# New x and block sums turned by DMA instead of TensorE at the inner boundaries of a two-layer encoder kernel, with the last tile's norm given priority and weight loads held behind the sums

## The chip, the cores and the metric

The kernel runs on one core of one Trainium2 chip. The metric is the device time of one execution in microseconds; before the change the median of three runs is 1997.66 us (1997.49 to 1998.72).

## What is computed

Two layers over x of 512 x 1024 float32; each layer is a feed-forward block ("f"), a token mixer ("m"), a second feed-forward block and a gated embedding block ("p"). Each ends in a layer norm of the sum of its input and its output, and that norm's result is the next block's x. In the reference, cut down:

```python
def reference(x, p, ...):
    for i in range(2):
        x = layer_norm(ALPHA * x + 0.5 * swiglu(x, ffn_w_in[i, 0], ffn_w_out[i, 0]), ...)
        x = layer_norm(ALPHA * x + token_mix(x, mix_w_in[i], ..., mix_w_out[i]), ...)
        x = layer_norm(ALPHA * x + 0.5 * swiglu(x, ffn_w_in[i, 1], ffn_w_out[i, 1]), ...)
        ple = sigmoid(x @ ple_w_gate[i] + ple_b_gate[i]) * (p[i] @ ple_w_proj[i])
        x = layer_norm(ALPHA * x + ple, ...)
    return x

def swiglu(x, w_in, w_out):                 # w_in 1024 x 5632, w_out 2816 x 1024
    gate, up = split(x @ w_in, 2)
    return (silu(gate) * up) @ w_out
```

## The kernel before, in words

The eight blocks run one after the other in the order f m f p, f m f p, so there are seven inner boundaries: f to m twice, m to f twice, f to p twice, p to f once. A Tile scheduler lists the instructions of each engine in a fixed order from the program and its priorities; on the chip each engine takes its own list in order and waits on semaphores. All loads and stores go through one queue, SP's, which also waits in order.

x stands in SBUF in four tiles of 128 tokens by 1024 (`x_tok`). A matmul needs x with the 1024 channels on the partitions, in two float16 parts whose sum is the float32 value: `xT`, high and low. A product is three matmuls, high by high, high by low, low by high (`mm3`, L270, L273, L274). So at each boundary every new tile of x is turned. Before the change that is done by `to_T` (L213): eight float32 128x128 transposes on TensorE (L224) into two PSUM banks `ps_t`, a copy on ScalarE to the high part (L229), a subtraction on VectorE for the low part (L230). `layer_norm` (L179) puts a tile on a list `pending`, and `flush` (L207) turns what is listed: the transposes of tile t stand on TensorE behind the output product of tile t+1, and those of the last tile in the next block.

A feed-forward block multiplies by Strassen's method in 2x2 blocks for hidden chunks 2 to 21 (`begin`, `step`), so it also needs four sums of blocks of x (`xS`, again two float16 parts). They are made from the transposed PSUM banks: a copy (L240), three to four subtractions (L246, L248), and `put_sums` (L255) with a copy on ScalarE (L262) and a subtraction on VectorE (L263). Chunks 0 and 1 use plain products; they are what TensorE has to do before the sums are there: `pg` and `pu` (the line of `project`), first for columns 0 to 384 of x (tiles 0 to 2), then for tile 3. The weight blocks of each chunk ("quad") are loaded to `f` (L470, L471), summed on VectorE (L484), and split in high and low by ScalarE (L141) and VectorE (L142) into `wq`. The output matrix comes in slabs `raw`, split by the same lines into `w`; `out_proj` (L492) runs per tile and group of chunks, ends in an eviction on VectorE (L517), and the norm of the tile follows (L185 to L197), with one small operation on GpSimd (L190). The last group of a feed-forward block has six chunks, that is 36 matmuls a tile.

The block p (L520) splits four slabs of `ple_w_gate` and one of `ple_w_proj` into `w`, multiplies tile by tile (`pgate`, then `pp`), and turns p itself by 16 TensorE transposes (`ps_p`, L550). Its slabs `w` lie in SBUF where the feed-forward block's buffers lay, so a split can wait for that block's last readers. In the mixer, `pv` (L653) is the first product, tile by tile.

Of the kernel before, what the change touches and what calls it, by code (L numbers as in the profile page):

```python
# [9 lines left out]
F16 = mybir.dt.float16  # L10
# [18 lines left out]

WS = 256.0  # L30
IWS = 1.0 / WS


class Block:
# [144 lines left out]
    def layer_norm(self, t, y, gb, last=False):  # L179

        nc = self.nc
        g, b = gb
        st = self.small.tile([P, 2, 6], F32, name="st")
        for h in range(2):
            nc.vector.bn_stats(st[:, h], y[:, h * 512 : (h + 1) * 512])  # L185
        mv = self.small.tile([P, 2], F32, name="mv")
        nc.vector.bn_aggr(mv, st.rearrange("p a b -> p (a b)"))
        rs = self.small.tile([P, 2], F32, name="rs")
        nc.vector.tensor_scalar(rs[:, 0:1], mv[:, 1:2], LN_EPS / ALPHA**2, None, op0=ALU.add)
        nc.gpsimd.tensor_tensor(rs[:, 1:2], rs[:, 0:1], self.mhalf[:, 0:1], op=ALU.pow)  # L190
        halves = [y[:, h * 512 : (h + 1) * 512] for h in range(2)]
        for h, yh in enumerate(halves):
            nc.vector.scalar_tensor_tensor(
                yh, yh, mv[:, 0:1], g[:, h * 512 : (h + 1) * 512], op0=ALU.subtract, op1=ALU.mult
            )
        for h, yh in enumerate(halves):
            nc.vector.scalar_tensor_tensor(  # L197
                yh, yh, rs[:, 1:2], b[:, h * 512 : (h + 1) * 512], op0=ALU.mult, op1=ALU.add
            )
# [13 lines left out]
    def to_T(self, xT, t, y, sums):  # L213
# [36 lines left out]
        if held is not None and t > 0:  # L250
            held.append(step)
        else:
            step()

    def put_sums(self, xS):  # L255

# [19 lines left out]
    def ffn(self, i, f, j, last=False):  # L276
# [7 lines left out]
        with ExitStack() as ctx:  # L284
# [37 lines left out]

            loads, loaded = [], []
            for m0, m1 in groups:
                loads += [lambda m=m: self.load_quad(w_in, m) for m in range(max(m0, 2), m1)]
                loads += [
                    lambda k=k, m=m0: (
                        self.load_rows(w_out, k, behind=self.chunks_end if first and m == 0 else None),
                        None,
                    ) for k in range(m0, m1, 2)  # L330
                ]

            def fetch(n):
                while loads and len(loaded) < n:
# [25 lines left out]
            for m in range(2):  # L360
                if m == 1:
                    self.put_sums(xS)
                ps = []
                for name, w in (("pg", wg), ("pu", wu)):
# [76 lines left out]
            for gi, (m0, m1) in enumerate(groups):  # L441
# [7 lines left out]
                wo = weights((m1 - m0) // 2)  # L449
                if gi == len(groups) - 1:  # L450
                    gb = self.ln_consts(i, j, self.w2, tag="w")
                for t in range(NT):
                    self.out_proj(
                        t, lambda q, m: hT[(m0 + m) // 2][:, q, m % 2], wo, m1 - m0,
# [1 line left out]
                    )  # L456
                    self.flush()
                    if gi == len(groups) - 1:
                        self.layer_norm(t, x[:, t], gb, last)

    def load_quad(self, w_in, m):


        nc = self.nc
# [5 lines left out]
        nc.sync.dma_start(f[:, 0:2], g)  # L470
        nc.sync.dma_start(f[:, 4:6], u)  # L471
        w = self.ring.tile([P, 2, 7, 4, P], F16, name="wq", tag="wq")

        def split(*slots):
# [45 lines left out]
    def ple(self, i, j, last=False):  # L520
        nc, ins, x, xT = self.nc, self.ins, self.x, self.xT
        self.xT = self.act.tile([P, 2, KD, S], F16, name="xT", tag="xT", bufs=2)
        with self.tc.tile_pool(name="ple", bufs=1, reuse_waits="tile") as pool, \
                self.tc.tile_pool(name="w1", bufs=5, reuse_waits="tile") as self.w1:
            pr = [self.t2("pr", (P, 2, 256)) for _ in range(2)]
            for h in range(2):
                nc.sync.dma_start(
                    pr[h], ins["p"][i, 0, 256 * h : 256 * h + 256].rearrange("(t p) e -> p t e", p=P)
                )
            wg = [self.load_rows(ins["ple_w_gate"][i], k, self.w1) for k in range(0, KD, 2)]  # L530
            wp = self.load_rows(ins["ple_w_proj"][i], 0, self.w1)
            bg = pool.tile([P, D], F32, name="bg")
            self.after(nc.sync.dma_start(bg, ins["ple_b_gate"][i : i + 1, :].to_broadcast([P, D])), self.loaded)
            gb = self.ln_consts(i, j, pool)
            pT = pool.tile([P, 2, 2, S], F16, name="pT")
            for t in range(NT):
                ts = slice(t * P, (t + 1) * P)
                pgs = [self.acc("pgate") for _ in range(2)]
                for h in range(2):
                    hs = slice(h * 512, (h + 1) * 512)  # L540
                    for m in range(KD):
                        self.mm3(
                            pgs[h], [xT[:, q, m, ts] for q in range(2)],
                            [wg[m // 2][:, q, m % 2, hs] for q in range(2)], m == 0, m == KD - 1,
                        )
                if t == 0:
                    for c in range(2):
                        ps = self.bank2("ps_p", (P, NT, P))
                        for tt in range(NT):
                            nc.tensor.transpose(  # L550
                                ps[:, tt], pr[tt // 2][:, tt % 2, c * P : (c + 1) * P], self.ident
                            )
                        hi = pT[:, 0, c].rearrange("p (t q) -> p t q", t=NT)
                        nc.scalar.activation(hi, ps, AF.Copy)
                        nc.vector.tensor_tensor(
                            pT[:, 1, c].rearrange("p (t q) -> p t q", t=NT), ps, hi,
                            op=ALU.subtract,
                        )
                self.flush()
                for h in range(2):  # L560
# [43 lines left out]
    def mix_body(self, i, j, last, pool):  # L604
# [7 lines left out]
        OFF_Q, OFF_K, OFF_V, OFF_Z, OFF_AB, OFF_SC = 768, 1280, 1792, 2304, 2816, 2824  # L612


        rows = self.t2("rows", (55, P))
        nc.sync.dma_start(rows[0:48], ins["gdn_conv_w"][i].rearrange("t (c p) -> (t c) p", p=P))
        nc.sync.dma_start(rows[48:54], ins["sc_conv_w"][i].rearrange("t (c p) -> (t c) p", p=P))
        nc.sync.dma_start(rows[54:55], ins["gdn_norm_w"][i : i + 1, :])
# [535 lines left out]
        for t in range(NT):  # L1154
            self.out_proj(t, lambda q, m: mT[:, q, m], wo, KD, IWS / ALPHA)
            self.flush()
            self.layer_norm(t, x[:, t], gb, last)

    def load_x(self):
        self.xT = self.act.tile([P, 2, KD, S], F16, name="xT", tag="xT", bufs=2)  # L1160
# [34 lines left out]
def encoder_block(ctx: ExitStack, tc: tile.TileContext, ins, out, stages="fmfp", layers=range(DEPTH)):  # L1195
# [2 lines left out]
    k.load_x()  # L1198
    for (i, j, s), following in zip(n, n[1:] + [None]):
        last = following is None  # L1200
        k.next_sums = not last and following[2] == "f"
        if s == "f":
            k.ffn(i, 0 if j == 0 else 1, j, last)
        elif s == "m":
# [25 lines left out]
```

## Time and profile before

| | |
|---|---|
| median of three runs | 1997.66 us |
| the profiled execution | 1997.14 us, span 1995.4 us |
| granted TensorE clock, mean over the span | 0.997 |
| VectorE busy | 76% of the span |
| ScalarE busy | 44% |
| bytes moved by DMA | 205.15 MB, 103 GB/s over the span |

The profile is of one execution. A row of the timeline has start, duration, engine, line, operation, output and inputs, size and count, and in brackets how long the engine had been idle and who released it. Matmuls overlap, so a matmul's own duration is longer than the step from its start to the next start; the step is what it costs. "PE" is TensorE, "PEld" its weight loads, "DVE" VectorE, "ACT" ScalarE, "POOL" GpSimd, "SPq" SP's queue.

### The profile page before, as it was taken

To read this page: it belongs to the slowest core of one execution; us is meant where nothing else is said; L and a number is where in the kernel's file an instruction comes from. 1 tells how busy PE (TensorE), PEld (TensorE's weight loads), DVE (VectorE), ACT (ScalarE), POOL (GpSimd) and SP (SyncE) were. 2 spreads that over 40 slices of the span, in tenths; PEclk is the share of its full clock that TensorE was granted. 3 is DMA by queue.
4 is the path that set the end of the run, shared out by engine and by line. 5 is a ranking of instruction groups with operands and counts; after the bars stand their busy time and mean duration, and the time that the engine had idled before them with its cause. 6 is when DMAs were issued, how large, how long until landed. Compare 5 with 4: busy or idle time off the path is not lost.

```text
span 1995.4 us, 33112 instructions
## 1 busy us (share of the span) xinstructions
PE 1951.3 (98%) x14058; PEld 1273.5 (64%) x14058; DVE 1521.9 (76%) x2347; ACT 868.1 (44%) x1294; POOL 69.9 (4%) x92
## 2 busy tenths in 40 slices
PE   8999999999999999999999999999999999999998
PEld 6677685545546677685467685854455466776853
DVE  8996766775679895869897877577756897967586
ACT  6454352454335453444264453424643364443430
POOL 1000000100000000000000000002000000000000
PEclk9999999999999999999999999999999999999999
DMA  8543320422162433334224343212222534333221
GB/s 243 181 127 106 86 86 14 117 56 64 65 197 79 148 106 106 106 120 148 92 85 127 106 126 84 66 55 78 53 86 80 174 97 136 106 106 85 96 74 43
DMA packets 245359, 205.15 MB, mean 103 GB/s; under 512 B 20846, under 2 KB 225500, under 8 KB 245212
## 3 DMA queue, kind: packets, MB, share of 16 engines
q1 hardware_dynamic: 245212, 203.05, 33.2%
q8 instruction: 110, 1.80, 0.4%
q14 instruction: 37, 0.30, 0.0%
HBM read 200.14 MB, written 2.88 MB: 102 GB/s over the span
## 4 chain that ended last, share of the span: by engine, by line
PE 75%; DVE 16%; ACT 6%; issue 2%; DMA 0%; POOL 0%; SPq 0%; DVEq 0%; ACTq 0%
PE po L274 7%; PE po L270 7%; PE po L273 7%; PE pA L270 6%; PE pA L273 6%; PE pA L274 6%; DVE wq L142 3%; PE pB L274 3%; PE pB L273 3%; PE pB L270 3%; DVE w L142 3%; ACT wq L141 2%; PE pC L270 1%; PE pC L273 1%; PE pC L274 1%
## 5 line engine op out<-in xcount | busy, mean ns | idle before, releaser
L142 DVE SCALAR_TENSOR_TENSOR wq<-f,wq 128x1024 f16<-128x1024 f32 (+1 forms) x240 | 334.2, 1395 | 18.8 <-ACT wq L141 15.6
L141 ACT ACTIVATE wq<-f 128x1024 f16<-128x1024 f32 (+1 forms) x240 | 279.4, 1191 | 126.6 <-PE pB L274 85.4
L141 ACT ACTIVATE w<-raw 128x1024 f16<-128x1024 f32 (+1 forms) x196 | 192.9, 1031 | 260.7 <-PE po L274 223.8
L270 PE MATMUL pA<-xS,wq 128*128 128x256 f16 x960 | 261.5, 272 | 7.6 <-ACT sg L439 3.9
L270 PE MATMUL po<-w,hT 128*128 128x512 f16 x704 | 266.9, 379 | 1.8 <-ACT hT L302 1.3
L274 PE MATMUL po<-w,hT 128*128 128x512 f16 x704 | 264.8, 379 | 2.7 <-DVE hT L303 2.7
L273 PE MATMUL po<-w,hT 128*128 128x512 f16 x704 | 266.8, 379 | 0.0
L274 PE MATMUL pA<-xS,wq 128*128 128x256 f16 x960 | 261.6, 273 | 0.0
L273 PE MATMUL pA<-xS,wq 128*128 128x256 f16 x960 | 261.6, 272 | 0.0
L142 DVE SCALAR_TENSOR_TENSOR w<-raw,w 128x1024 f16<-128x1024 f32 (+1 forms) x196 | 229.6, 1193 | 36.0 <-ACT w L141 35.9
L273 PEld LDWEIGHTS <-wq 128*128 128x128 f16 x2240 | 219.1, 98 | 44.3 <-issue 14.1
L484 DVE TENSOR_TENSOR f<-f 128x512 f32<-128x512 f32 x320 | 219.1, 687 | 26.2 <-DMA f<-in_ffn_w_in 21.1
L270 PEld LDWEIGHTS <-wq 128*128 128x128 f16 x2240 | 219.1, 98 | 30.3
L274 PEld LDWEIGHTS <-wq 128*128 128x128 f16 x2240 | 219.1, 98 | 26.9
L517 DVE SCALAR_TENSOR_TENSOR x_tok<-po,x_tok 128x512 f32<-128x512 f32 x144 | 97.3, 685 | 82.9 <-PE po L274 82.9
L274 PEld LDWEIGHTS <-hT 128*128 128x128 f16 x704 | 68.0, 98 | 86.2 <-DVE hT L303 6.5
L420 DVE TENSOR_TENSOR sg<-pB,sg 128x256 f32<-128x256 f32 x80 | 33.7, 421 | 115.7 <-PE pB L274 115.7
L270 PEld LDWEIGHTS <-hT 128*128 128x128 f16 x704 | 68.9, 98 | 79.7 <-ACT hT L302 3.4
L439 ACT ACTIVATE sg<-pA 128x256 f32<-128x256 f32 x80 | 30.5, 382 | 203.7 <-PE pA L274 203.7
L273 PEld LDWEIGHTS <-hT 128*128 128x128 f16 x704 | 68.9, 98 | 77.0 <-issue 1.1
L273 PEld LDWEIGHTS <-w 128*128 128x128 f16 x640 | 62.7, 98 | 61.8 <-issue 14.1
L270 PEld LDWEIGHTS <-w 128*128 128x128 f16 x640 | 62.7, 98 | 59.7 <-issue 5.4
(290 smaller groups left out, 3823.4 us busy)
## 6 DMA issues: line engine op xcount, KB each, us to landing
f<-in_ffn_w_in SPq DMA_DIRECT2D x160, 512.0 KB, 5.0
raw<-in_ffn_w_out SPq DMA_DIRECT2D x44, 1024.0 KB, 6.1
raw<-in_mix_w_in SPq DMA_DIRECT2D x28, 1024.0 KB, 5.5
raw<-in_mix_w_out SPq DMA_DIRECT2D x8, 1024.0 KB, 5.0
raw<-in_ple_w_gate SPq DMA_DIRECT2D x8, 1024.0 KB, 6.0
raw<-in_ffn_w_in SPq DMA_DIRECT2D x6, 1024.0 KB, 5.8
ln_gb<-in_ln_g SPq DMA_DIRECT2D x8, 512.0 KB, 3.9
ln_gb<-in_ln_b SPq DMA_DIRECT2D x8, 512.0 KB, 4.7
```

The source lines that it names most:

```text
L141: self.nc.scalar.activation(hi, raw, AF.Copy, scale=WS),
L142: self.nc.vector.scalar_tensor_tensor(lo, raw, WS, hi, op0=ALU.mult, op1=ALU.subtract),
L270: begun = nc.tensor.matmul(ps, a[0], b[0], start=first, stop=False, **k)
L273: nc.tensor.matmul(ps, a[0], b[1], start=False, stop=False, **k)
L274: return nc.tensor.matmul(ps, a[1], b[0], start=False, stop=last, **k)
L420: nc.vector.tensor_tensor(half(old.sg, 1), old.B, half(old.sg, 1), op=ALU.add)
L439: nc.scalar.activation(half(u.sg, 1), u.A, AF.Copy)
L484: total = nc.vector.tensor_tensor(f[:, to], f[:, a], f[:, b], op=ALU.add)
L517: self.nc.vector.scalar_tensor_tensor(xs, po[h], scale, xs, op0=ALU.mult, op1=ALU.add)
```

## The change

At all inner boundaries new x is turned by DMA: `pair_T` copies a tile to float16 (high) on ScalarE, subtracts (low) on VectorE, both from SBUF and 1024 wide, and issues two DMA transposes on SP's queue into `xT`. Ahead of f and m the last tile still goes over TensorE; ahead of p all four go by DMA. The sums for a feed-forward block are made from `x_tok` in token order (`turn_sums`) and go through `pair_T` as well, eight transposes for each block that has a boundary in front of it. p is loaded early and turned by DMA in the preceding block's last group (`load_early`), which takes the tile `pT` out of p's own pool; the mixer's small `rows` are loaded there too. The last tile's norm is emitted with high priority (`norm_tile`). The quad of chunk 5, and the output slabs of the group that begins at chunk 4, are kept behind the last sums' transposes on SP. The first products of a feed-forward block are cut at column 256 instead of 384. Two new pools, `tmp4` and `early`, take SBUF ahead of the others.

```diff
@@ class Block
+        self.tmp4 = pool("tmp4", bufs=2)
+        self.early = pool("early", bufs=1)
...
         if not last:
-            self.pending.append((self.xT, t, y, self.next_sums))
+            self.turn(self.xT, t, y)
+
+    def norm_tile(self, t, gb, last):
+        if t == NT - 1 and not last:
+            with self.tc.high_priority(offset=400):
+                self.layer_norm(t, self.x[:, t], gb)
+        else:
+            self.layer_norm(t, self.x[:, t], gb, last)
...
+    def pair_T(self, out, pieces, wide=False):
+        nc = self.nc
+        hi, lo = (self.t2("turn", (P, D), F16) for _ in range(2))
...
+            nc.scalar.activation(h, y, AF.Copy)
+            nc.vector.tensor_tensor(l, y, h, op=ALU.subtract)
+        for q, v in enumerate((hi, lo)):
+            self.sent = nc.sync.dma_start_transpose(out(q), v)
+
+    def turn(self, xT, t, y):
+        kind = self.following[2]
+        if kind not in KINDS or kind != "p" and t == NT - 1:
+            self.pending.append((xT, t, y, kind not in KINDS and kind == "f"))
+        else:
+            self.pair_T(lambda q: xT[:, q, :, t * P : (t + 1) * P], y, wide=True)
+
+    def load_early(self):
...
+        if kind == "p":
+            pr = self.tmp4.tile([P, NT, 256], F32, name="pr", tag="ts")
+            nc.sync.dma_start(pr, ins["p"][i, 0].rearrange("(t p) e -> p t e", p=P))
+            pT = self.pT = self.tmp4.tile([P, 2, 2, S], F16, name="pT", tag="ts")
...
+    def turn_sums(self, xS, a):
...
+        one, two = (self.tmp4.tile([P, 2, 512], F32, name="ts", tag="ts") for _ in range(2))
+        first = nc.vector.tensor_tensor(one[:, 0], b11, b12, op=ALU.subtract)
+        if a:
+            self.after(first, self.turned[1])
+        for to, p, m in (
+            (one[:, 1], b22, one[:, 0]), (two[:, 0], one[:, 1], b11), (two[:, 1], one[:, 1], b21)
+        ):
+            nc.vector.scalar_tensor_tensor(to, p, -1.0, m, op0=ALU.mult, op1=ALU.subtract)
+        for n, ts in ((0, one), (2, two)):
+            self.pair_T(
+                lambda q: xS[:, q, n : n + 2].rearrange("p n k c -> p (n k) c")[:, :, a * P : (a + 1) * P],
+                ts.rearrange("p n c -> p (n c)"), wide=True,
+            )
...
@@ def ffn
+                if m == 4 and not first:
+                    self.after(self.loaded, sums_sent)
...
-                done = project(*args, 0, 384, done if first and n else None)
+                done = project(*args, 0, 384 if first else 256, done if first and n else None)
...
+            if not first:
+                self.turn_sums(xS, 0)
+                for args in ahead:
+                    project(*args, 256, 384)
             self.flush()
-            self.put_sums(xS)
+            if first:
+                self.put_sums(xS)
+                sums_sent = None
+            else:
+                self.turn_sums(xS, 1)
+                sums_sent = self.sent
...
                     gb = self.ln_consts(i, j, self.w2, tag="w")
+                    if not last:
+                        self.load_early()
...
@@ def load_quad
+        for dma in (nc.sync.dma_start(f[:, 0:2], g), nc.sync.dma_start(f[:, 4:6], u)):
+            if behind is not None:
+                self.after(dma, behind)
...
@@ def ple
-            pr = [self.t2("pr", (P, 2, 256)) for _ in range(2)]
...
-            pT = pool.tile([P, 2, 2, S], F16, name="pT")
+            pT = self.pT
...
-                            nc.tensor.transpose(
-                                ps[:, tt], pr[tt // 2][:, tt % 2, c * P : (c + 1) * P], self.ident
-                            )
```

What moves is best seen in the engines' lists. The first place is VectorE at the first boundary from f to p. Before, from the norm of tile 0 on; `x_tok<-po` is the eviction of half a tile (9047 and 9067 tile 1, 9113 tile 2), `w` a split of a slab of p's weights (9275 and 9282 the last two of the gate, 9289 the projection), the rows with `ln_gb` the norm:

```order
L142 SCALAR_TENSOR_TENSOR w_9275<-raw_9273,w_9275 128x1024
L189 TENSOR_SCALAR rs_9040<-mv_9038 128x1
L193 SCALAR_TENSOR_TENSOR x_tok_140<-x_tok_140,mv_9038,ln_gb_8992 128x512 x2
L197 SCALAR_TENSOR_TENSOR x_tok_140<-x_tok_140,rs_9040,ln_gb_8992 128x512 x2
L517 SCALAR_TENSOR_TENSOR x_tok_140<-po_9047,x_tok_140 128x512
L142 SCALAR_TENSOR_TENSOR w_9282<-raw_9280,w_9282 128x1024
L517 SCALAR_TENSOR_TENSOR x_tok_140<-po_9067,x_tok_140 128x512
...
L142 SCALAR_TENSOR_TENSOR w_9282<-raw_9280,w_9282 128x1024
L187 BN_AGGR mv_9104<-st_9101 128x2
L142 SCALAR_TENSOR_TENSOR w_9289<-raw_9287,w_9289 128x1024
```

And now, from the eviction of the last half tile (9230 is tile 3's second half; the gate's slabs are 9280, 9287, 9294, 9301, the projection 9308):

```order
L613 SCALAR_TENSOR_TENSOR x_tok_146<-po_9230,x_tok_146 128x512
L188 BN_STATS st_9250<-x_tok_146 128x6
L145 SCALAR_TENSOR_TENSOR w_9280<-raw_9278,w_9280 128x1024
L190 BN_AGGR mv_9253<-st_9250 128x2
L145 SCALAR_TENSOR_TENSOR w_9280<-raw_9278,w_9280 128x1024
L192 TENSOR_SCALAR rs_9255<-mv_9253 128x1
L196 SCALAR_TENSOR_TENSOR x_tok_146<-x_tok_146,mv_9253,ln_gb_9022 128x512 x2
L200 SCALAR_TENSOR_TENSOR x_tok_146<-x_tok_146,rs_9255,ln_gb_9022 128x512 x2
L145 SCALAR_TENSOR_TENSOR w_9287<-raw_9285,w_9287 128x1024 x2
L279 TENSOR_TENSOR turn_9263<-x_tok_146,turn_9262 128x1024
L145 SCALAR_TENSOR_TENSOR w_9294<-raw_9292,w_9294 128x1024 x2
L145 SCALAR_TENSOR_TENSOR w_9301<-raw_9299,w_9301 128x1024 x2
```

All ten half splits of p's weights have moved from beside the last output products to behind them. With `pT` out of p's pool, the first slab (9280) now lies over the hidden chunks `hT` that the last output product reads, and ScalarE's half of its split waits for that product.

The second place is SP's list at the same boundary; it was, with the gate's last slab and the projection next to each other:

```order
L527 DMA pr_9255<-in_p 128x2x256
L527 DMA pr_9256<-in_p 128x2x256
L161 DMA raw_9280<-in_ple_w_gate 128x2x1024
L161 DMA raw_9287<-in_ple_w_proj 128x2x1024
L150 DMA raw_9741<-in_ffn_w_in 128x8x256
```

It is now, from tile 2's turning on (9204 and 9205 are its high and low part, 9262 and 9263 tile 3's):

```order
L281 DMA_TRANSPOSE xT_5894<-turn_9204 128x8x128
L281 DMA_TRANSPOSE xT_5894<-turn_9205 128x8x128
L176 DMA ln_gb_9315<-in_ln_g 128x1024
L177 DMA ln_gb_9315<-in_ln_b 128x1024
L164 DMA raw_9299<-in_ple_w_gate 128x2x1024
L281 DMA_TRANSPOSE xT_5894<-turn_9262 128x8x128
L164 DMA raw_9306<-in_ple_w_proj 128x2x1024
L281 DMA_TRANSPOSE xT_5894<-turn_9263 128x8x128
```

The last two slabs now stand behind transposes that wait for the norms of tiles 2 and 3, and behind the norm's constants, which wait for the same chunks `hT`.

The third place is VectorE at the first boundary from m to f, behind the last tile's transposes on TensorE. Before (`ts` are sums, `xS` their low parts, `wq` a quad's split):

```order
L230 TENSOR_TENSOR xT_5634<-ps_t_6049,xT_5634 128x4x128
L230 TENSOR_TENSOR xT_5634<-ps_t_6056,xT_5634 128x4x128
L246 TENSOR_TENSOR ts_6063<-ts_5931,ps_t_6049 128x512
L142 SCALAR_TENSOR_TENSOR wq_6280<-f_6277,wq_6280 128x1024
L248 SCALAR_TENSOR_TENSOR ts_6064<-ps_t_6056,ts_6063 128x512
L263 TENSOR_TENSOR xS_5949<-ts_6063,xS_5949 128x4x128
```

And now (`turn` 6103 and 6104 are the high and low part of the first two sums, 6109 and 6110 of the other two):

```order
L240 TENSOR_TENSOR xT_5616<-ps_t_6083,xT_5616 128x4x128
L240 TENSOR_TENSOR xT_5616<-ps_t_6090,xT_5616 128x4x128
L317 TENSOR_TENSOR ts_6097<-x_tok_146 128x512
L145 SCALAR_TENSOR_TENSOR wq_6310<-f_6307,wq_6310 128x1024
L323 SCALAR_TENSOR_TENSOR ts_6097<-x_tok_146,ts_6097 128x512
L145 SCALAR_TENSOR_TENSOR wq_6310<-f_6307,wq_6310 128x1536
L323 SCALAR_TENSOR_TENSOR ts_6098<-ts_6097,x_tok_146 128x512 x2
L279 TENSOR_TENSOR turn_6104<-ts_6097,turn_6103 128x1024
L145 SCALAR_TENSOR_TENSOR wq_6310<-f_6307,wq_6310 128x1024
L279 TENSOR_TENSOR turn_6110<-ts_6098,turn_6109 128x1024
```

The sums' low parts went straight into `xS`; now they go to a buffer, and a DMA has to land before TensorE can read them.

More of the change, by code (lines that the diff above doesn't have):

```diff
@@ L31 @@
 IWS = 1.0 / WS
+KINDS = "mpf"
 class Block:
@@ L253, in to_T @@
             step()
+    def pair_T(self, out, pieces, wide=False):
+        nc = self.nc
+        hi, lo = (self.t2("turn", (P, D), F16) for _ in range(2))
+        if wide:
+            pieces, n = [pieces], D
+        else:
+            n = 512
+        for c, y in enumerate(pieces):
+            h, l = (v[:, c * n : (c + 1) * n] for v in (hi, lo))
+            if len(y.shape) == 3:
+                h, l = (v.rearrange("p (a b) -> p a b", b=y.shape[2]) for v in (h, l))
+            nc.scalar.activation(h, y, AF.Copy)
+            nc.vector.tensor_tensor(l, y, h, op=ALU.subtract)
+        for q, v in enumerate((hi, lo)):
+            self.sent = nc.sync.dma_start_transpose(out(q), v)
@@ new lines, in turn @@
+    def turn(self, xT, t, y):
[5 more added lines that the diff above has]
+    def load_early(self):
+        nc, ins = self.nc, self.ins
+        i, j, kind = self.following
+        if kind == "m":
+            rows = self.rows = self.early.tile([55, P], F32, name="rows", tag="rows")
+            nc.sync.dma_start(rows[0:48], ins["gdn_conv_w"][i].rearrange("t (c p) -> (t c) p", p=P))
+            nc.sync.dma_start(rows[48:54], ins["sc_conv_w"][i].rearrange("t (c p) -> (t c) p", p=P))
+            nc.sync.dma_start(rows[54:55], ins["gdn_norm_w"][i : i + 1, :])
+        if kind == "p":
[3 more added lines that the diff above has]
+            self.pair_T(
+                lambda q: pT[:, q].rearrange("p c (t k) -> p (c t) k", k=P),
+                [pr[:, :, c * P : (c + 1) * P] for c in range(2)],
+            )
@@ new lines, in turn_sums @@
+    def turn_sums(self, xS, a):
+        nc = self.nc
+        b11, b21, b12, b22 = (
+            self.x[:, 2 * a + t, 512 * h : 512 * h + 512] for t in range(2) for h in range(2)
+        )
+        one, two = (self.tmp4.tile([P, 2, 512], F32, name="ts", tag="ts") for _ in range(2))
[7 more added lines that the diff above has]
+        for n, ts in ((0, one), (2, two)):
+            self.pair_T(
+                lambda q: xS[:, q, n : n + 2].rearrange("p n k c -> p (n k) c")[:, :, a * P : (a + 1) * P],
+                ts.rearrange("p n c -> p (n c)"), wide=True,
+            )
@@ L324, in ffn @@
             for m0, m1 in groups:
-                loads += [lambda m=m: self.load_quad(w_in, m) for m in range(max(m0, 2), m1)]
+                loads += [
+                    lambda m=m: self.load_quad(w_in, m, sums_sent if m == 5 else None)
+                    for m in range(max(m0, 2), m1)
+                ]
                 loads += [
                     lambda k=k, m=m0: (
-                        self.load_rows(w_out, k, behind=self.chunks_end if first and m == 0 else None),
+                        rows(k, m),
                         None,
@@ L331, in ffn, with rows @@
                 ]
+            def rows(k, m):
+                w = self.load_rows(w_out, k, behind=self.chunks_end if first and m == 0 else None)
+                if m == 4 and not first:
+                    self.after(self.loaded, sums_sent)
+                return w
             def fetch(n):
@@ L360, in ffn @@
             for m in range(2):
-                if m == 1:
+                if m == 1 and first:
                     self.put_sums(xS)
@@ L458, in ffn, with load_quad @@
                     if gi == len(groups) - 1:
-                        self.layer_norm(t, x[:, t], gb, last)
-    def load_quad(self, w_in, m):
+                        self.norm_tile(t, gb, last)
+    def load_quad(self, w_in, m, behind=None):
         nc = self.nc
@@ L612, in mix_body @@
         OFF_Q, OFF_K, OFF_V, OFF_Z, OFF_AB, OFF_SC = 768, 1280, 1792, 2304, 2816, 2824
[L615 to L618, printed above, removed]
+        rows = self.rows
         hd = sm.tile([P, 2, 2], F32, name="hd", bufs=1)
@@ L1156, in mix_body @@
             self.flush()
-            self.layer_norm(t, x[:, t], gb, last)
+            self.norm_tile(t, gb, last)
     def load_x(self):
@@ L1200, in encoder_block @@
         last = following is None
-        k.next_sums = not last and following[2] == "f"
+        k.following = following
         if s == "f":
```

17 lines of the change are left out of this document (1 added, 16 removed).

## The prediction

> **What bounds the kernel now.** I read the page first: span, busy times, the chain that ended last.
>
> ```profile
> span 1995.4 us, 33112 instructions
> PE 1951.3 (98%) x14058; PEld 1273.5 (64%) x14058; DVE 1521.9 (76%) x2347; ACT 868.1 (44%) x1294; POOL 69.9 (4%) x92
> PE 75%; DVE 16%; ACT 6%; issue 2%; DMA 0%; POOL 0%; SPq 0%; DVEq 0%; ACTq 0%
> ```
>
> TensorE is busy for 98% of the span, so what is taken from it shortens the kernel, as long as VectorE, a sixth of the chain, does not take its place. Next came the table of windows (sum, then busy PE, PEld, DVE, ACT, POOL, granted clock, DMA share, GB/s), one row in the first feed-forward block and one behind the boundary from m to f.
>
> ```profile
> 200.00:300.00 100.00, 99.45 (x769) 74.84 (x767) 72.51 (x104) 43.01 (x64) 2.07 (x4) 1.00 0.30 86
> 600.00:700.00 100.00, 97.35 (x699) 65.27 (x698) 89.20 (x127) 47.79 (x67) 1.97 (x2) 1.00 0.34 108
> ```
>
> In the middle of a block VectorE has a quarter free; where a feed-forward block starts it is at 89%, and a wait that appears there is not recovered soon. The clock is full in both. Then the groups by line, for TensorE's transposes, and TensorE's timeline for what one costs.
>
> ```profile
> L224 PE MATMUL ps_t<-ident,x_tok 128*128 128x128 f32 x256 | 35.7, 285 | 7.7 <-POOL masks L74 4.6 <-DVE x_tok L197 3.0
> 604.08 1.04 PE L224 MATMUL ps_t<-ident,x_tok 128*128 128x128 f32 x8
> 604.95 0.38 PE L270 MATMUL po<-w,mT 128*128 128x512 f16 x1
> ```
>
> Eight transposes move the next matmul by 0.87 us, 0.108 each; the 285 ns are overlapped. The group waits for tokens only 3.0 us in all.
>
> **The change, part by part.** *TensorE.* Of the 256, 72 stay (four tiles at the start, the last tile ahead of f and m five times); 184 go, and the 16 of `ps_p`: 200 by 0.108 are 21.7 us, the most that the change can bring. Whether it arrives depends on each boundary. Below, T is the start of TensorE's first work behind the last output product; instructions are counted along the new lists with durations from rows of before. DMA transposes are in no row of before. Call L their time from issue to landing, for 256 KB. The nearest rows:
>
> ```profile
> out<-x_tok SPq DMA_DIRECT2D x8, 256.0 KB, 2.0
> f<-in_ffn_w_in SPq DMA_DIRECT2D x160, 512.0 KB, 5.0
> raw<-in_ple_w_gate SPq DMA_DIRECT2D x8, 1024.0 KB, 6.0
> TU<-dx SPq DMA_DIRECT2D x16, 32.0 KB, 2.3
> ```
>
> The low end is 2.0, the same bytes plainly stored; the far end is 18, if each eighth cost what the 32 KB copy does (8 x 2.3). The quad's load, whole 5.0 and by half its bytes 2.5, comes in runs of 128 columns, as the turned blocks have them, so it is nearest: I take L = 3.5 and keep 2 to 5 for the forecast's own case.
>
> [...]
>
> *f to m (twice).*
>
> ```profile
> 340.55 1.04 PE L224 MATMUL ps_t<-ident,x_tok 128*128 128x128 f32 x8
> 347.89 1.29 PE L224 MATMUL ps_t<-ident,x_tok 128*128 128x128 f32 x8 [0.91 <-DVE x_tok L197]
> 343.21 1.28 DVE L230 TENSOR_TENSOR xT<-ps_t,xT 128x512 f16<-128x512 f32 x2
> ```
>
> The first row is tile 2's turning at T, the second tile 3's, which TensorE reaches early and waits for the norm. Tiles 0 and 1 (1.74) go before T. At the wait, tile 2's 0.87 would only be replaced by waiting, but the norm's chain also loses the low part in the third row, 1.2. Gain 2.9 each. Tile 2's transposes are issued before T and needed 8 us behind it, so L up to 8 costs nothing here.
>
> *m to f (twice).*
>
> ```profile
> 615.31 1.04 PE L224 MATMUL ps_t<-ident,x_tok 128*128 128x128 f32 x8
> 616.72 0.32 PE L270 MATMUL pg<-xT,w 128*128 128x384 f16 x1 [0.38 <-ACT xT L229]
> 628.78 1.04 PE L224 MATMUL ps_t<-ident,x_tok 128*128 128x128 f32 x8
> 640.36 0.27 PE L270 MATMUL pB<-xS,wq 128*128 128x256 f16 x1
> 623.20 4.02 DVE L142 SCALAR_TENSOR_TENSOR wq<-f,wq 128x1024 f16<-128x1024 f32 x3
> 635.38 1.89 DVE L263 TENSOR_TENSOR xS<-ts,xS 128x512 f16<-128x512 f32 x3
> ```
>
> Before, the first product with a sum stands at T+25.05, and the low parts of the sums are written from T+20.1. Now 1.74 goes before T, and tile 2's 0.87 with the 0.54 of waiting at T go too (1.4; cutting 384 into 256 and 128 costs 0.16 by the matmul steps). Counted at equal work TensorE would be 1.5 earlier, but the list brings it to a product with sums at T+19.85, since 5.2 of `pu` now stands behind. The last sums are later than that: tile 3's transposes at T+12.2 (the third row's T+13.5 less the 1.4, plus 0.16) and turned 2.4 later (four steps of 0.60) at T+14.6, sums with the split that stands between them (0.60 and 1.13 a step) T+16.9, high part on ScalarE, which has a quad's splits ahead of it, T+19.5, DMA issued T+19.6, landed T+19.6+L. TensorE stalls L-0.25. So -1.74 -1.5 +3.25 = 0 at L = 3.5, and each us of L costs one.
>
> *p to f (once).*
>
> ```profile
> 1001.34 0.33 PE L270 MATMUL pg<-xT,w 128*128 128x384 f16 x1
> 1014.56 1.29 PE L224 MATMUL ps_t<-ident,x_tok 128*128 128x128 f32 x8 [1.14 <-DVE x_tok L197]
> 1027.11 0.27 PE L270 MATMUL pB<-xS,wq 128*128 128x256 f16 x1
> ```
>
> Three tiles (2.6) go before T; T+25.8 becomes, by the same steps, 0.5 earlier at L = 3.5, the last sums landing at T+18.1+L. Together -3.1, again one per us of L.
>
> *f to p (twice).*
>
> ```profile
> 943.45 1.04 PE L224 MATMUL ps_t<-ident,x_tok 128*128 128x128 f32 x8
> 957.09 0.39 PE L270 MATMUL pp<-w,pT 128*128 128x512 f16 x1 [0.82 <-ACT pT L554]
> 960.95 0.38 PE L274 MATMUL pgate<-w,xT 128*128 128x512 f16 x1
> 941.06 3.90 ACT L141 ACTIVATE w<-raw 128x1024 f16<-128x1024 f32 x4 [4.53 <-PE po L274]
> 943.14 1.21 DVE L142 SCALAR_TENSOR_TENSOR w<-raw,w 128x1024 f16<-128x1024 f32 x1
> 944.28 0.68 DVE L185 BATCH_NORM_STATS2 st<-x_tok 128x6 f32<-128x512 f32 x1
> 944.88 0.67 DVE L517 SCALAR_TENSOR_TENSOR x_tok<-po,x_tok 128x512 f32<-128x512 f32 x1
> 950.80 1.40 DVE L193 SCALAR_TENSOR_TENSOR x_tok<-x_tok,mv,ln_gb 128x512 f32<-128x512 f32 x2
> 952.12 1.40 DVE L197 SCALAR_TENSOR_TENSOR x_tok<-x_tok,rs,ln_gb 128x512 f32<-128x512 f32 x2
> ```
>
> Saved: before T two tiles and some of `ps_p`, 2.07. Before, tile 0's `pp`, which begins in the second row, is through when TensorE goes on with tile 1's `pgate` in the third, T+17.5; 1.24 of that is `pgate` of tile 1 done in between, so T+16.3 at equal work. The change puts the splits of p's weights behind T: the first slab overlies chunks that the last output product reads, ScalarE's split waits for it, later ones queue behind. VectorE's list then reads: eviction and statistics (two by 0.60), two splits (1.13 each), the last norm (1.32 twice) to T+6.5; two splits T+8.8; low part and two splits T+12.1; two more T+14.4. The projection's load stands on SP behind tile 3's high transpose, is issued at T+8.9, takes 6.0, and its splits end at T+18.3; tile 0 ends at T+19.2. That is 2.9 later, less 2.07: +0.8 each.
>
> *The rest.* The quad of chunk 5 waits for the last sums' DMA, and later loads queue behind it on SP. TensorE spends 9.1 us on a quad (84 matmuls of 0.108), and it is needed three quads after the sums; landing takes 5.0: nothing, as long as L stays under some 10 us. The turning's VectorE work is near equal (sums and low parts from SBUF at 0.60 per 512 columns, as from PSUM). Early p and `rows` loads are covered by the output products: nothing, and if late at most the 0.82 that `pp` waits for p now.
>
> The sum: 2 x (-2.9) + 0 - 3.1 + 2 x 0.8 = -7.3 at L = 3.5, against the profiled execution's 1997.14 (the median is 0.5 above it): 1989.8, say 1990. With three per us of L: -11.8 at 2, -2.8 at 5, nothing won at 5.9.
>
> **The rivals.** *The whole saving arrives.* The stalls of L-0.25 and the splits behind T are counted along lists with estimates good to perhaps 1.5 us a boundary; if TensorE has other products to run at each, 21.7 comes off: 1975. For it: TensorE waits little at boundaries now. Against: VectorE at 89%.
>
> *The transposes are slow.* The same mechanism with L beyond 5.9, so at three boundaries TensorE waits at the first product with sums: L = 8 gives +6.2, 2003; L = 10.5 gives +13.7, 2011; at 18, the far row, +36 and chunk 5's quad late besides. For it: no row above is of a DMA that turns, and a copy of 32 KB already takes 2.3. Against: 256 KB stored takes 2.0. [...]
>
> *p's splits cost more than they save.* Ten half splits in a row by 1.13 behind the last norm are 11.3 us of VectorE in the stretch where TensorE needs them in order.
>
> ```profile
> L142 DVE SCALAR_TENSOR_TENSOR w<-raw,w 128x1024 f16<-128x1024 f32 (+1 forms) x196 | 229.6, 1193 | 36.0 <-ACT w L141 35.9
> ```
>
> In this group VectorE waits almost only for ScalarE's half. If that half comes later than assumed, by one slab (two ScalarE steps and two splits, some 4 us), f to p costs +4.8 each instead of 0.8: +0.7 in all, 1997.8, and the change gives back what it saves. Against: ScalarE needs about 1.0 a half and is 44% busy.
>
> **How the numbers follow.** A measurement of this kernel tells about 0.2% (4 us) from no change. The forecast with L from 2 to 5, 1985 to 1995, gets 0.45: faster 0.36, same 0.09. The whole saving, 1975: 0.20, faster. Slow transposes: 0.20, slower 0.17, same 0.03. p's splits: 0.15, same 0.10, slower 0.05. Sums: 0.56, 0.22, 0.22. The likeliest is 1990. The range goes from just under the whole saving, 1974, to 2008, between L = 8 and 10.5; left out are the longest landings.
>
> **What would show it.** Right: a row of DMA transposes with 2 to 5 us from issue to landing; TensorE with some 1930 us busy (1951.3 less 21.7); at both m to f a wait of 2 to 5 us on `xS` by DMA; p's tile 0 done 19 us behind T. Wrong, upward: landings of 8 us and more, waits on `xS` of the same size, or waits on `w` at the start of p over 6 us. Wrong, downward: no wait on `xS`, and VectorE's backlog absorbed. If the whole time does not move although 200 transposes are gone from the count and all landings are short, the bound was VectorE, and the argument from TensorE's 98% falls.

## The result and the profile after

The changed kernel takes 2012.42 us (median of four runs, 2011.77 to 2013.31), the kernel before 1997.58 beside it: ratio 1.0074, 95% interval 1.0062 to 1.0086. The forecast was 1990, faster; it came out slower by 14.8 us.

First the page: span, busy times, the chain, and the landing times of the new DMAs.

```profile
span 2010.1 us, 33218 instructions
PE 1941.8 (97%) x14074; PEld 1267.8 (63%) x14074; DVE 1524.5 (76%) x2312; ACT 862.0 (43%) x1247; POOL 69.8 (3%) x92
...
xT<-turn SPq DMA_TRANSPOSE x46, 3.2
...
xS<-turn SPq DMA_TRANSPOSE x24, 3.3
```

The landing time L is 3.2 to 3.3, where the forecast took 3.5. TensorE is busy for 9.5 us less, not 21.7, although all 200 transposes are gone (next row: 72 are left); six stretches at half clock, 23.9 us in all, in which a float16 matmul of 128 columns steps by 0.107 us instead of 0.056, stretch the rest of its work by up to half of that, 11.9. The transposes did what they were to do; the time went elsewhere.

```profile
L234 PE MATMUL ps_t<-ident,x_tok 128*128 128x128 f32 x72 | 12.2, 323 | 6.9 <-POOL masks L77 4.7 <-ACT ts L250 1.2 <-DVE x_tok L200 1.0
```

The windows show where. The columns are window, length, busy PE, PEld, DVE, ACT, POOL, granted clock, DMA share, GB/s; the short windows lie at the first m to f.

```profile
200.00:300.00 100.00, 99.45 (x768) 74.83 (x766) 72.56 (x104) 43.07 (x64) 2.07 (x4) 1.00 0.30 85
600.00:700.00 100.00, 92.38 (x698) 64.42 (x697) 83.67 (x113) 41.08 (x53) 1.97 (x2) 0.97 0.57 158
627.30:630.70 3.40, 0.00 (x0) 0.00 (x0) 1.29 (x3) 3.40 (x4) 0.00 (x0) 1.00 0.23 65
630.70:634.10 3.40, 3.34 (x32) 3.34 (x32) 3.40 (x6) 0.48 (x2) 0.00 (x0) 0.50 0.00 0
651.20:654.60 3.40, 1.09 (x11) 0.82 (x10) 2.70 (x5) 2.55 (x4) 0.00 (x0) 1.00 1.16 296
654.60:658.00 3.40, 3.40 (x19) 2.34 (x17) 3.30 (x6) 0.00 (x0) 0.00 (x0) 0.50 1.06 400
```

Inside a block nothing changed (first row). At the boundary VectorE is not fuller but emptier than before, 83.7 against 89.2: it waits too. And each of two waits of TensorE is followed by 3.4 us at half clock. The waits themselves, on TensorE (in brackets idle time and who ended it):

```profile
613.00 0.27 PE L345 MATMUL pg<-xT,w 128*128 128x256 f16 x1
...
624.88 1.04 PE L234 MATMUL ps_t<-ident,x_tok 128*128 128x128 f32 x8
630.76 0.27 PE L348 MATMUL pg<-xT,w 128*128 128x128 f16 x1 [3.61 <-DVE xT L240]
639.31 0.39 PE L345 MATMUL pB<-xS,wq 128*128 128x256 f16 x2 [0.99 <-DMA xS<-turn]
...
654.26 0.27 PE L345 MATMUL pA<-xS,wq 128*128 128x256 f16 x1 [2.31 <-ACT up L527]
```

Only the second was in the forecast, and it is smaller than the 3.25 there. The first is for the low part of the last tile, which VectorE makes. VectorE's own rows show why it is late:

```profile
623.76 2.35 DVE L145 SCALAR_TENSOR_TENSOR w<-raw,w 128x1024 f16<-128x1024 f32 x2
629.41 0.69 DVE L580 TENSOR_TENSOR f<-f 128x512 f32<-128x512 f32 x1 [3.29 <-DMA f<-in_ffn_w_in]
630.02 1.28 DVE L240 TENSOR_TENSOR xT<-ps_t,xT 128x512 f16<-128x512 f32 x2
```

One block sum of chunk 4's quad (L580) stands ahead of the low part in VectorE's list and waits 3.29 us for its load. Before, the first of these sums stood far behind, at 642.93. The third wait, on ScalarE and SP's queue:

```profile
651.94 2.00 ACT L144 ACTIVATE w<-raw 128x1024 f16<-128x1024 f32 x2 [2.82 <-DMA raw<-in_ffn_w_out]
653.85 0.36 ACT L527 ACTIVATE up<-pA 128x256 f32<-128x256 f32 x1
```

```profile
634.81 5.50 SPq L281 DMA_TRANSPOSE xS<-turn  x3
...
641.02 1.24 SPq L281 DMA_TRANSPOSE xS<-turn  x1
642.31 2.13 SPq L565 DMA_DIRECT2D f<-in_ffn_w_in  x2
644.48 1.08 SPq L164 DMA_DIRECT2D raw<-in_ffn_w_out  x1
```

The slab that is kept behind the last sums is issued at 644.48 and lands at 651.94, 7.5 us later; the output slabs (`raw<-in_ffn_w_out`) land in 7.1 us here by the median, against 6.1 before and 5.9 and 6.3 in the runs free and both below, in which nothing is held: the hold also bunches the loads. ScalarE stands at its split, and the small copy behind it (`up`), which would free TensorE's accumulator, is late by that much.

By stages: the table gives, in us against before, how much later (or earlier) the same matmul starts at the end of a stage than at its beginning, in the profiled executions. The runs in the columns are told below; the inside of the feed-forward blocks is 0.0 in all of them. The column "changed" adds up to +14.5 where -7.3 was forecast. A stage that an edit leaves alone can still move (f to p to f from +3.6 to +4.7 under "both", the second mixer from -0.1 to +1.7 under "after m"), so a single difference of 1 us is weak evidence.

| stage | forecast | changed | order | free | both | pad | three edits | m and p | after m | copy |
|---|---|---|---|---|---|---|---|---|---|---|
| f to m, 1st | -2.9 | -3.0 | -3.0 | -3.0 | -3.0 | -3.0 | -3.0 | -3.0 | -3.0 | -3.0 |
| mixer, 1st | 0 | +2.4 | +2.2 | +2.9 | +2.8 | +2.2 | +4.7 | +3.1 | +2.0 | +1.0 |
| m to f, 1st | 0 | +5.9 | +2.3 | +5.0 | -1.1 | +5.7 | -1.3 | +0.6 | -0.9 | -1.2 |
| f to p to f | -2.3 | +3.6 | +4.7 | +4.5 | +4.7 | -3.4 | -2.6 | -4.6 | -4.6 | -4.6 |
| f to m, 2nd | -2.9 | -3.0 | -3.0 | -3.0 | -3.0 | -3.0 | -3.0 | -3.0 | -3.0 | -3.0 |
| mixer, 2nd | 0 | -0.1 | -0.1 | -0.1 | -0.2 | -0.1 | -0.1 | 0.0 | +1.7 | +0.7 |
| m to f, 2nd | 0 | +6.0 | +1.8 | +4.7 | -1.6 | +5.5 | -1.3 | +0.6 | -1.6 | -1.4 |
| f to p, 2nd | +0.8 | +2.7 | +2.7 | +2.7 | +2.7 | -3.4 | -3.4 | -3.4 | -3.4 | -3.4 |

### The profile page after: what moved, and what is told of

Same layout as the page of the kernel before. It is cut to its first block, busy times and chain, and to the rows that moved or that the text cites. A ratio compares the mean times of both kernels' runs of the same rounds, so it can differ in the third digit from the quotient of the medians.

```text
span 2010.1 us, 33218 instructions
## 1 busy us (share of the span) xinstructions
PE 1941.8 (97%) x14074; PEld 1267.8 (63%) x14074; DVE 1524.5 (76%) x2312; ACT 862.0 (43%) x1247; POOL 69.8 (3%) x92
## 5 line engine op out<-in xcount | busy, mean ns | idle before, releaser
L580 DVE TENSOR_TENSOR f<-f 128x512 f32<-128x512 f32 x320 | 220.0, 689 | 40.4 <-DMA f<-in_ffn_w_in 34.8
L349 PEld LDWEIGHTS <-w 128*128 128x128 f16 x712 | 70.3, 99 | 62.7 <-issue 12.2
L348 PEld LDWEIGHTS <-w 128*128 128x128 f16 x712 | 70.4, 99 | 59.0 <-issue 15.0
```

The source lines that it names most:

```text
L348: nc.tensor.matmul(ps, a[0], b[1], start=False, stop=False, **k)
L349: return nc.tensor.matmul(ps, a[1], b[0], start=False, stop=last, **k)
L580: total = nc.vector.tensor_tensor(f[:, to], f[:, a], f[:, b], op=ALU.add)
```

## The experiments

The theory after the result: the transposes are as quick as forecast, and three things that the lists make take the gain and more: a block sum that waits for its load ahead of the last tile's low part, loads held behind the sums, and p's splits behind the last output product; the half clock adds to the longer waits. The rival: VectorE's work at the start of a block is the bound, and taking one wait away only brings the next. Another: transposes and loads hinder each other in the DMA engines.

**order** (label e1_order): chunk 4's block sums behind the last tile's turning.

```diff
-                if self.opening and self.quads < 4:
+                if (self.opening or self.quads == 2) and self.quads < 4:
                     self.after(total, self.turned[1])
```

> One edit: the block sums of chunk 4's quad stand on VectorE behind the last tile's low part, in every feed-forward block. Theory (the order of the lists makes waits, and TensorE's clock falls to half after the longer ones): at the first m to f the wait of 3.88 us for the low part shrinks to about 1.2 (ScalarE's high part, then 0.6 of VectorE) and the half-clock stretch at 630.7 (3.41 us, worth 1.7) does not come; at the second the 3.55 shrink likewise, with no half-clock stretch to save. In all -5 to -7 us from 2012.4, about 2006. Rival (VectorE's work at the start of a block is the bound, whatever its order): the wait comes back at the sums, within 2 us of 2012.4.

Measured: 2005.31 us (median of four runs from 2004.34 to 2010.3), ratio to before 1.0045 (1.0028 to 1.0062), 7.1 less than the changed kernel. The wait for the low part is gone; at the first m to f the wait for the sums is the first that is left:

```profile
634.69 0.39 PE L345 MATMUL pB<-xS,wq 128*128 128x256 f16 x2 [1.92 <-DMA xS<-turn]
```

The stage fell from +5.9 to +2.3 and from +6.0 to +1.8. So the rival that only moves waits does not hold for this one.

**free** (e2_free): no load waits for the sums.

```diff
-                    lambda m=m: self.load_quad(w_in, m, sums_sent if m == 5 else None)
+                    lambda m=m: self.load_quad(w_in, m)
...
-                if m == 4 and not first:
-                    self.after(self.loaded, sums_sent)
```

> One edit: the quad of chunk 5 and the output slabs of the group from chunk 4 on wait no longer for the last sums' transposes. Theory: the waits of 2.58 and 3.96 us for ScalarE, which stands at a split of a late slab, go at m to f, and 1.43 at p to f, with the half-clock stretches behind them (654.6, and 6.83 us at 1647.9): up to -13 us; but in the new list all four block sums of chunk 4 stand ahead of the last tile's low part, which adds up to 1.8 at each m to f, so -6 to -10, about 2004. Rival (VectorE's work is the bound): within 2 us of 2012.4. Rival (transposes and loads hinder each other in the DMA engines): slower, since more loads run beside the sums' transposes.

Measured: 2010.71, ratio 1.0063 (1.0048 to 1.0078): 1.7 less, well short of what the theory gave. The slab's waits went, but four block sums now stand ahead of the low part (TensorE still waits 2.48 us for it at the first m to f), the wait for the sums grew from 0.99 to 1.39, and TensorE waits 1.68 more for an accumulator that ScalarE frees. By itself this edit shows little; the next run shows it with the sums out of the way.

**both** (e3_order_free): the two edits together.

> Both edits of the two runs before. Theory: of the three waits at m to f only that for the sums' transposes is left (1.3 us or a little more), and no half-clock stretch behind the others: the sum of both, -13 to -17 us from 2012.4, about 1997. Rival (VectorE's work is the bound): -2 to 0, since the waits only move.

Measured: 1999.24, ratio 1.0007 (0.9998 to 1.0017), 13.2 less. At both m to f one wait is left, the one for the sums:

```profile
635.46 0.38 PE L345 MATMUL pB<-xS,wq 128*128 128x256 f16 x2 [1.83 <-DMA xS<-turn]
```

The stages are -1.1 and -1.6, below the 0 of the forecast. VectorE does the same work as in the changed kernel, so its work was not the bound at m to f. More loads beside the sums' transposes did not slow them either: they land in 3.3 us, as in the changed kernel.

**pad** (e4_pad): p's pool gets 4 KB a partition that nothing uses, where the turned p stood.

```diff
             gb = self.ln_consts(i, j, pool)
+            pad = pool.tile([P, 2, 2, S], F16, name="pad")
+            nc.gpsimd.memset(pad[:, 0, 0, 0:1], 0.0)
             pT = self.pT
```

> One edit: 4 KB a partition that nothing uses are put back into p's pool where its turned p stood, so that the first slab of p's weights no longer lies over the chunks that the last output product reads; all ten half splits then stand beside the last output products again, as before the change. Theory: behind T only the last norm and its turning are left on VectorE, tile 0 of p is done about 14 us behind T instead of 19.7, no half-clock stretch at 955: -5 us at each f to p, -10 in all, about 2002. Rival (VectorE has no room beside the last output products, so the evictions come late and TensorE waits there): under -4.

Measured: 1998.76, ratio 1.0004 (0.9994 to 1.0013), 13.7 less, more than expected: f to p falls from +2.7 to -3.4 in the second layer, and in the first by 7.0 with p to f. The last tile's eviction is now all that TensorE waits for at T:

```profile
947.91 0.38 PE L345 MATMUL pgate<-w,xT 128*128 128x512 f16 x1 [0.53 <-DVE x_tok L613]
```

All ten half splits end by 944.6, ahead of T, and TensorE's list begins p with `pp` (946.58): VectorE has the room beside the output products. What cost here was where a buffer lay, not the turning.

**three edits** (e5_all): order, free and pad.

> The three edits together: chunk 4's block sums behind the last tile's low part, loads not held behind the sums, p's pool padded so that its first slab lies clear of the last chunks. Theory (separate waits at separate boundaries): the gains add, 2012.4 - 13.2 - 13.7, about 1985.5. Rival (VectorE's work is the bound and each edit only moves the wait): well short of the sum, 1992 or more.

Measured: 1986.72, ratio 0.9944 (0.9927 to 0.996). The gains add to within 1.2 us (1985.5 expected): separate waits at separate places. By the table the rest was lost in the first mixer, +4.7 against +2.8 under "both".

**m and p** (e6_only_mp): the DMA turns x only ahead of m and p; ahead of f all is as before the change.

```diff
-        if kind not in KINDS or kind != "p" and t == NT - 1:
-            self.pending.append((xT, t, y, kind not in KINDS and kind == "f"))
+        if kind == "f" or kind != "p" and t == NT - 1:
+            self.pending.append((xT, t, y, kind == "f"))
...
-            if not first:
-                self.turn_sums(xS, 0)
...
             self.flush()
+            self.put_sums(xS)
```

> New x is turned by DMA only ahead of m and p (with p's pool padded); ahead of f, x and its sums go over TensorE and PSUM as before the change, with no held loads and the cut at 384. Theory (turning by DMA pays ahead of m and p, 3.0 and about 3.4 us each time, and brings nothing ahead of f): 1997.7 - 6.0 - 6.8, plus about 2 that the first mixer loses in all versions with the new lists: about 1987, within 2 of the run with the three edits. Rival (the sums by DMA are a gain once their lists are mended): 4 us or more slower than that run.

Measured: 1986.81, ratio 0.9946 (0.9932 to 0.9961): no different from the three edits, as expected, but by differences that cancel: by DMA m to f is 1.9 better each time, and f to p to f 2.0 worse; the rest is the first mixer.

**after m** (e9_mix_only): so the sums go by DMA only where f follows m.

```diff
-        if kind not in KINDS or kind != "p" and t == NT - 1:
+        old = kind == "f" and self.following[1] == 0
+        if old or kind != "p" and t == NT - 1:
```

> The run with the three edits, but ahead of the f that follows p, x and the sums go over TensorE and PSUM as before the change; by DMA they go only where f follows m. By stages of the two runs before: m to f -1.3 each by DMA against +0.6 over TensorE, p to f +0.8 by DMA against -1.2 over TensorE. Theory (the two boundaries differ, since p's last products leave the sums' chain less cover): 2.0 under the run with the three edits, about 1984.7. Rival (the stages' differences are chance shifts of the clock's stretches): no difference.

Measured: 1984.44, ratio 0.9935 (0.992 to 0.995), 2.3 under the three edits. The stage f to p to f is 2.0 better, as expected. The first mixer is 2.7 better and the second 1.8 worse, which no sum had; that these nearly cancel is luck, so the stage supports the theory better than the whole time does.

**sums first** (e8_sums_first): the three edits, and chunk 3's splits on VectorE behind the sums' low parts.

```diff
                 self.turn_sums(xS, 1)
+                self.turned = (self.turned[0], self.low)
```

> The three edits together, and chunk 3's splits on VectorE behind the last sums' low parts, where two of them (1.13 and 1.67 us) stand between the sums. Theory (what is left at m to f and p to f is the sums' chain on VectorE and its landing): the waits of 2 to 3 us for the sums' transposes shrink by up to 2.8 each, -4 to -6 against the run with the three edits alone. Rival (chunk 3's quad is needed just behind): the wait moves to its weights, 0 or slower.

Measured: 1986.45, ratio 0.9945 (0.993 to 0.996): nothing gained in all. By stages f to p to f is 1.4 better than with the three edits (-4.0), and the two m to f are 1.5 and 0.6 worse (+0.1 and -0.7). At the first, TensorE's wait for the sums is 2.22 us instead of 1.83, and a half-clock stretch follows at 636.8. The theory left out ScalarE: VectorE now waits for it, 0.69 and 0.66 us, since it still has a quad's splits ahead of the sums' high part.

```profile
628.71 3.38 ACT L144 ACTIVATE wq<-f 128x1024 f16<-128x1024 f32 x3
631.98 1.05 ACT L278 ACTIVATE turn<-ts 128x1024 f16<-128x1024 f32 x1
```

**filler** (e7_filler): 64 matmuls added at both m to f of the changed kernel, into columns that the next product begins anew.

```diff
+                for _ in range(64):
+                    prev, fill = fill, nc.tensor.matmul(
+                        ps[:, 384:512], w[:, 0, 0, 0:P], xT[:, 0, 0, 0:P], start=True, stop=True
+                    )
+                    self.after(fill, prev)
```

> The changed kernel with 64 matmuls of 128 columns added at both m to f, right behind the last tile's transposes on TensorE, 3.6 us of work into columns that the next product begins anew; they fill most of the waits of 3.88 and 3.55 us for that tile's low part, so that the half-clock stretch at 630.7 should not come. If each such stretch costs its 1.7 us: -1.7 of 2012.4. If it costs only where nothing else waits behind it: here the wait for the sums' transposes follows, which land at a time that TensorE doesn't set, so the time stays within 0.5 and that wait grows from 1.26 to about 2.9. If the work of TensorE itself is the bound: +3 to +7.

Measured: 2020.06, ratio 1.0115 (1.01 to 1.013), slower by 7.6 than the changed kernel. The half-clock stretch at 630.7 did not come. The next wait, 2.70 us from start to start, has the size that the second case gave, but it is not the wait for the sums. TensorE's list came out in another order, with a product `pu` ahead of the first one that needs a sum, and it waits there for an accumulator that ScalarE frees behind the sums' high parts:

```profile
638.88 0.38 PE L345 MATMUL pu<-xT,w 128*128 128x512 f16 x1 [2.43 <-ACT sg L474]
```

That wait drew a stretch of its own at 640.2, and more waits follow (to 661.7 and 666.3, with a stretch at 667.5). The two m to f are 3.7 and 3.3 worse than in the changed kernel, about the 3.6 of the added work. Since the list changed with the edit, the run settles none of the three cases, nor what the half clock costs by itself.

**copy** (e10_act_copy): the run "after m", and a copy in the mixer by ScalarE instead of VectorE.

```diff
-                nc.vector.tensor_copy(ks[other, h], ks[own, h])
+                nc.scalar.activation(ks[other, h], ps[own], AF.Copy, scale=IWS)
```

> The kernel of the run beside it, and in the mixer the copy of ks from one half of the partitions to the other, which VectorE makes from SBUF, is made by ScalarE from PSUM. Theory (that copy, 0.29 us when alone, ends 0.40 us behind GpSimd's multiplication of 2.35 us whenever it starts during it, and TensorE then waits over 2.5 us before the sum of the gates): the wait at 406 us falls to about 1.5 and no half-clock stretch follows, -1 to -2.5 us. Rival (that stretch waits for something else, or ScalarE is no earlier): 0, or slower by up to 1.

Measured: 1982.02, ratio 0.9924 (0.9908 to 0.9941), 2.4 under the run beside it, and the fastest of all; 1.0 of it in each mixer by the table. This edit has no tie to the change; no run has it in the kernel before. The start-to-start wait near 406 fell from 2.40 to 1.34; there was no half-clock stretch in either run, so the half clock has no part in this gain.

No run takes away the priority of the last tile's norm, the early loads of p, or the cut at 256 by itself; what they are worth stays open.

## Why the prediction was wrong, point by point

Between the forecast's -7.3 and the +14.5 of the table lie 21.8 us: 11.9 at the two m to f, 5.9 at the first f to p with p to f, 1.9 at the second f to p, and 2.4 in the first mixer; the small rest goes the other way.

*L.* Right: 3.2 to 3.3 where 3.5 was taken, and the stalls behind it were smaller than forecast at m to f. The rival of slow transposes gave nearly the measured time (2011 at L = 10.5) by a mechanism that isn't there. No run shows the 10.5, which the upper end of the range rests on too; in its place the 74 DMA transposes land in 3.1 to 3.3 by the medians of their three groups, and a plain store of 256 KB takes 2.1 in this run.

*f to m.* Right: -3.0 twice, where -2.9 was forecast. Of the first, though, 2.4 is given back inside the mixer, which the forecast left at nothing: 1.1 near 370, where ScalarE's split of a weight slab, which waits for its load, is only 1.6 us earlier than before though TensorE is there 3.0 earlier, and most of the rest at the copy told below.

*m to f.* This is the step that failed: 0 was forecast, with one stall of 3.25; measured are +5.9 and +6.0. At the first, the stall for the sums came out smaller (0.99). In its place: 3.61 for the low part behind a block sum, 2.31 for a slab, and at most 3.4 us in two half-clock stretches (half of 2 x 3.41). Together up to 10.3; less 2.6 of transposes and some 1.6 of waits that before had here makes 6.1. Two steps in the working were at fault. The chain "tile 3 turned at T+14.6" counted VectorE's list from the low part on and left out the row in front of it; it was T+18.2. And "the quad of chunk 5 waits ... nothing" priced the quad and not the slabs that are held with it. Chunk 4's slabs are split long before their products, but on an engine that works in order, with TensorE's accumulators behind. With both mended, the stage is -1.1 and -1.6, and the stall for the sums 1.83 at the first: the sum for the sums by DMA was right within 2 us, on the cautious side.

*p to f.* From T on -0.5 was forecast; the same matmul at T is 5.2 late and in mid-block 9.0, so +3.7. The stall for the sums is 2.28, a half-clock stretch behind it takes up to 1.7, and a second wait, again behind a late slab on ScalarE, 1.16. No run isolates these: with the loads freed, f to p to f was no better (+4.5 and +4.7). The first of them in the profile:

```profile
1029.16 0.39 PE L345 MATMUL pB<-xS,wq 128*128 128x256 f16 x2 [2.28 <-DMA xS<-turn]
```

*f to p.* The chain on VectorE was counted right to 0.3 us at each step. From T = 947.06:

```profile
952.30 1.41 DVE L200 SCALAR_TENSOR_TENSOR x_tok<-x_tok,rs,ln_gb 128x512 f32<-128x512 f32 x2
953.62 2.36 DVE L145 SCALAR_TENSOR_TENSOR w<-raw,w 128x1024 f16<-128x1024 f32 x2
955.89 1.22 DVE L279 TENSOR_TENSOR turn<-x_tok,turn 128x1024 f16<-128x1024 f32 x1
957.03 4.63 DVE L145 SCALAR_TENSOR_TENSOR w<-raw,w 128x1024 f16<-128x1024 f32 x4
962.85 2.36 DVE L145 SCALAR_TENSOR_TENSOR w<-raw,w 128x1024 f16<-128x1024 f32 x2 [1.20 <-ACT w L144]
```

The norm ends at T+6.6 (forecast 6.5), the splits at 8.8 (8.8), 12.3 (12.1), 14.6 (14.4) and 18.1 (18.3). The term was mis-sized at its base: in the second layer tile 0 of p is done at T+15.25 before the change, without the wait of 0.82 that the first layer has, and only 1.76 is saved before T, not 2.07; with T+19.7 now that is 4.45 - 1.76, the +2.7 measured. The rival on p's splits named the right place, but by another mechanism, a ScalarE half that comes late, and with 4.8 where 2.7 was measured. That the cover lay there to be had again, by 4 KB, the forecast didn't ask.

*The bound.* The working held TensorE's 98% for a bound that takes what is removed. Inside the blocks that is so (0.0 in all runs). At the boundaries it is the order of VectorE's, ScalarE's and SP's lists: three edits that take no work off any engine turned 2012.42 into 1986.72. What would have helped is in the order itself: to read the rows in front of the place quoted, and to ask of each row there what it waits for.

## What to carry to other kernels

When work is moved off the busiest engine, price the boundary by the three lists that feed it, from some ten rows ahead of the place: one instruction there that waits for a load holds everything behind it (3.29 us here). Price each load that is held back by the first instruction that splits it, on an engine that works in order (2.82 us of waiting on ScalarE here), not by the product that needs it. And when a tile leaves a pool, look at what now lies over what: here 4 KB of padding were worth 13.7 us.

## What the runs showed of the hardware

**Half clock.** In the changed kernel all stretches at half clock begin whole multiples of 3.413 us apart (from 630.70 to 654.59 seven of them, to 408.83 back 65), and last one or two such steps. They follow windows of that grid in which TensorE was busy for 1.35 us or less (or one that itself ran at half clock). After 1.43 (the window from 1948.2) and 1.67 the clock stayed full, so the third longest wait inside the kernel (3.27 us, shared by two windows) drew none:

```profile
1620.60:1624.00 3.40, 1.67 (x16) 1.25 (x15) 0.83 (x1) 3.33 (x5) 0.00 (x0) 1.00 0.89 247
1624.00:1627.40 3.40, 1.82 (x33) 1.82 (x33) 3.17 (x5) 1.96 (x3) 0.00 (x0) 1.00 0.00 0
...
405.40:408.80 3.40, 1.35 (x7) 0.49 (x5) 3.21 (x12) 2.01 (x4) 0.00 (x0) 1.00 0.00 0
408.80:412.20 3.40, 3.20 (x12) 1.59 (x12) 3.27 (x11) 3.01 (x5) 0.00 (x0) 0.50 0.00 0
```

So a window that is 60% idle is enough (1.35 of 3.40 busy). The border isn't sharp: before the change the window of 3.41 us from 8.99, with 1.52 busy, drew a stretch, where 1.43 drew none here. One stretch stands outside this: at 370.5 in three runs (three edits, sums first, filler) it follows a window with 2.1 to 2.4 us of busy time, part of it matmuls of 16 columns; why is open. A stretch takes up to 1.7 us (half of 3.41, by the steps of 0.107 and 0.056), and it can take nothing: tile 0 of p ends at T+19.7 in both layers, with a stretch at 955.0 in the first and none in the second, since TensorE waits there for VectorE's splits. In the first mixer the runs with one such stretch lose 2.4 to 3.1 (changed, free, both, m and p), those without it 2.0 to 2.2 (order, pad, after m): so of 1.7 some 0.2 to 1.1 seems to come through there, as far as runs with different lists can be compared. The three edits lose 4.7 there, with two stretches and a copy of 2.59 us.

**A copy that ends behind GpSimd.** VectorE's copy of ks takes 0.29 us, and 2.41 where it starts during an operation of GpSimd:

```profile
398.81 2.41 DVE L932 COPY ks<-ks 64x512 f16<-64x512 f16 x1 [3.99 <-ACT ks L931]
...
402.59 0.29 DVE L932 COPY ks<-ks 64x512 f16<-64x512 f16 x1 [0.66 <-ACT ks L931]
```

```profile
398.47 2.35 POOL L1032 TENSOR_TENSOR E<-E,mask 128x1024 f32<-128x1024 f32 x1 [4.01 <-PE psb L349]
```

It ends 0.40 behind GpSimd's (0.15 to 0.40 in the other runs); before the change it took 1.40, since GpSimd's operation had begun earlier beside it. Why it takes so long these rows don't show. A kernel that is shifted by 3 us can so lose 1 us in a place that nobody touched.

**Issue of a DMA transpose.** The four behind the sums of the first m to f hold SP's queue for 1.23 to 1.30 us each; by the median over the kernel it is 1.24 for `xT` and 1.29 for `xS`, against 0.57 for a quad's load and 0.37 for a slab of the output matrix:

```profile
L281 SPq DMA_TRANSPOSE xS<-turn x4: 1232/1244/1297, 634.8 to 641.0; - x4
```

Four of them are 5 us of SP's queue just where the next block's loads stand behind them.
